# TensorE takes the instructions of one stage in traced order: attention, mLSTM and the first output projection of a two-layer hybrid backbone

## The chip, the core and the metric

The kernel runs on one core of one Trainium2 chip. The metric is device time in microseconds (us), here the median of three runs. The engines are TensorE (PE; its weight loads are shown apart as PEld), VectorE (DVE), ScalarE (ACT), GpSimd (POOL), and SyncE (SP), which issues most DMAs. All of them run at once, each through its own queue, and they wait for one another by semaphores.

## What is computed

Two layers of a hybrid backbone run over 256 context tokens and 1024 latent tokens of width 1024. Cut to what matters here, one layer is:

```python
hl = rms_norm(x_lat, norm1_g) * (1.0 + sc1) + sh1
zl = split_cols(hl @ w_in)
s5 = s5_mixer(...)
ml = mlstm_mixer(...)            # chunks of 128 tokens, both directions, 4 heads
da = diff_attention_mixer(...)   # w = softmax(s1) - lam * softmax(s2); o = w @ v
gl = gla_mixer(...)
x_lat = x_lat + g1 * (concatenate([s5, ml, da, gl]) @ w_out)
x_lat = x_lat + g2 * sq_relu_mlp(rms_norm(x_lat, norm2_g) * (1.0 + sc2) + sh2)
```

Context tokens go through the same layer, but not through the outputs of the last one.

## The kernel before, in words

The kernel is one long unrolled program, written in generators that are traced in turn. A traced instruction goes to the queue of its engine, and the scheduler of the programming layer then sets the order within each queue. It models the run, and whenever an engine comes free in its model it takes, of the instructions whose inputs are ready there, the one that was traced first. So a queue may leave the traced order wherever the model found the next traced instruction not ready. What comes out is a fixed order: on the chip each engine takes its queue from the front.

A layer has these stages: input projections, beside S5 and gated linear attention (GLA); then attention, mLSTM and the first half of the output projection, which is the stage of the change; then the second half of the output projection and the MLP.

In the stage of the change three generators are traced side by side (lines 1485 to 1499):

- `da_mix` (line 442), differential attention. For each head and each tile of 128 queries, `scores` multiplies queries by keys into PSUM (`daps`, L486), once for each of two maps and in up to three pieces of up to 512 keys. DVE takes each piece out with a running minimum (`das`, L487), ACT takes the exponential (L498), and DVE combines the two maps (L506). `values` then transposes the weights (`dapt`, L527), ACT copies them out (`dawT`, L528), and `dapo` (L518) multiplies them by the values. Score pieces go to three PSUM banks: two are called "a", the third piece has "x".
- `ml_mix` (line 690), the mLSTM. Transposes of the keys (`mlpt`, L756), state products (`mlpu`, L788), scores (`mlst`, L804), values (`mlpn`, L821 and L826), and, for each pair of chunks, `finish` (line 837): POOL and ACT and DVE normalise a tile `mlhs`, and two transposes (`mlpt`, L853) turn it. `mlhs` has one buffer.
- `p_out` (line 1465), the output projection of the S5 and GLA halves. For each 256 columns (a chunk of columns) `mix_parts` (line 1437) loads four pieces `mr` through two buffers (L1443), and ACT and DVE split each into a high part `mh` (L1444) and a low part `ml` (L1445), which have one buffer each; then eight output tiles follow, each of twelve matmuls `wop` (L1124 to L1126) whose weights `whl` are loaded and split, and each is taken out by ACT (`pg`, L1480). There are five such chunks in the first layer and four in the second.

The traced order around the change comes from two helpers. `both(da, 1, ml, 0.25)` (line 1218) traces one step of mLSTM to four steps of attention. `beside(..., po, 0.12)` (line 1135) traces one output tile, twelve `wop`, to about every eight steps of attention, and the first of them after the very first score matmul, since the credit is then already above zero. `dapt`, `wop` and the small attention products share the two PSUM banks "b".

Of the kernel before, what the change touches and what calls it, by code (L numbers as in the profile page):

```python
# [1091 lines left out]
ENG = dict(P=mybir.EngineType.PE, V=mybir.EngineType.DVE, A=mybir.EngineType.Activation, G=mybir.EngineType.Pool, S=mybir.EngineType.SP)  # L1092
# [42 lines left out]
def beside(main, filler, rate, guard=contextlib.nullcontext):  # L1135

    credit = 0.0
    for c in main:
        credit += rate * c
        if credit > 0:  # L1140
            with guard():
                while credit > 0:
                    credit -= next(filler, 1e9)
# [69 lines left out]
def both(a, na, b, nb):  # L1213

    ca = cb = 0.0
    for x in a:
        yield x
        ca += 1
        while cb / nb < ca / na:
            next(b, None)  # L1220
            cb += 1
# [44 lines left out]
def tile_hybrid_backbone(ctx: ExitStack, tc: tile.TileContext, io, out):  # L1266
# [49 lines left out]
    def pool(nm, side=None):  # L1316
        p = tc.tile_pool(name=nm, bufs=1, side=side, reuse_waits="tile") if side else tc.tile_pool(name=nm, bufs=1, reuse_waits="tile")
        return p, p.__enter__()

    def shut(p):  # L1320
        p.__exit__(None, None, None)
# [42 lines left out]
    for l in range(L):  # L1364
# [8 lines left out]
        if l == 0:  # L1373

            npc, P = pool("nx0", "right")
# [28 lines left out]
        def put(i):  # L1404
            def cb(m, t, c0):
                (nc.sync, nc.scalar, nc.sync, nc.sync)[i].dma_start(mix_d[i, m, :, c0:c0 + t.shape[1]], t)
            return cb
# [3 lines left out]
        if l == 0:  # L1411
            ready(("dak1",))
            spc, P = pool("s5p0")
# [52 lines left out]
        def p_out(P):  # L1466

            w = 256
            for b in blocks:
                t0, t1 = BLK[b]  # L1470
                for c in range(t0, t1, w):
                    n = min(w, t1 - c)
                    g1 = mod(l, 2, b == 0)
                    parts = mix_parts(P, c, n, 0, w)
                    for m in range(8):
                        x = P.tile([128, w], F32, tag="xo", name="xo", bufs=2)
                        nc.sync.dma_start(x[:, :n], x_d[:, m, c:c + n])
                        p = out_proj(m, n, 0, parts, c == BLK[blocks[0]][0])
                        pg = P.tile([128, w], F32, tag="pg", name="pg", bufs=1)
                        nc.scalar.mul(pg[:, :n], p, g1[:, m:m + 1])  # L1480
                        nc.gpsimd.tensor_tensor(x[:, :n], x[:, :n], pg[:, :n], op=ALU.add)
                        nc.sync.dma_start(xn_d[:, m, c:c + n], x[:, :n])
                        yield n / 256
# [5 lines left out]
        poc, P = pool(f"po{l}")  # L1489
        po = p_out(P)  # L1490
        da = da_mix(env, l, st, zd["dav"], io["da_lam"][l], 0.8 - 0.6 * math.exp(-0.3 * l), io["da_ng"][l], env.bones, put_da, need)
        mgc, MG = pool(f"mlg{l}", "right")
        mgates = ml_gates(env, l, MG, zd["gates"], io["ml_gb"][l], io["amask"], io["hsel"])
        ml = ml_mix(env, l, mgates, lambda i: zd[("mlq0", "mlq1", "mlk0", "mlk1")[i]], zd["mlv"], zd["mlo"], io["ml_cw"][l], io["ml_cb"][l],
                    io["ml_ng"][l], io["cmask"], put(1), need)
        beside((1 for _ in both(da, 1, ml, 0.25)), po, 0.12)
        list(ml)
        shut(mgc)
        list(po)
        env.banks.update(BANKS)  # L1500
        shut(ps2c)
        ps2c = banks(f"ps2{l}")
# [13 lines left out]
        woc, P = pool(f"wo{l}", "right")  # L1516
# [20 lines left out]
        hdc, P = pool(f"hid{l}", "right")  # L1537
# [76 lines left out]
    fnc, P = pool("fin")  # L1614
# [98 lines left out]
```

## Time and profile before

| | us |
|---|---|
| median of three runs (lowest, highest) | 3724.48 (3724.34, 3726.04) |
| the profiled execution, own time | 3719.97 |
| its span, first to last instruction | 3718.2 |
| busy: PE matmul, PE weight load | 3435.5, 2725.4 |
| busy: DVE, ACT, POOL | 2228.8, 1309.4, 450.7 |

The durations below come from the one profiled execution. Matmuls are pipelined and their ends are modelled, so a busy PE is not PE at its peak. The stage of the change runs from about 640 to 1013 us in the first layer and from about 2582 to 2915 us in the second. In rows of the timeline, "[0.80 <-DVE mlhs L849]" says that the engine stood idle for 0.80 us and what ended that.

### The profile page before, as it was taken

Reading aid. Unit: us, or ns where it says so; the run is one execution under the profiler, and the core shown is the slowest. Engines: PE = TensorE matmul, PEld = TensorE weight load, DVE = VectorE, ACT = ScalarE, POOL = GpSimd, SP = SyncE. Lnnn points to the kernel's source line nnn. Section 1 sums busy time; section 2 is a strip of 40 time slices with the busy share of each in tenths; the row PEclk is TensorE's granted clock in tenths of the full one; section 3 lists DMA queues with packets and bytes.
Section 4 is the critical chain, followed back from the end, with each engine's and each line's share of the span. In section 5 each row is a group of like instructions: output and inputs, shape, how many; then the busy total and the mean of one; then the engine's idle time right before and its main releaser. Section 6 shows DMA issues by size and latency. Waiting matters only on the chain. (4 is left out here: it accounts for less than half of the span.)

```text
span 3718.2 us, 53487 instructions
## 1 busy us (share of the span) xinstructions
PE 3435.5 (92%) x20338; PEld 2725.4 (73%) x20338; DVE 2228.8 (60%) x5455; ACT 1309.4 (35%) x2457; POOL 450.7 (12%) x520
## 2 busy tenths in 40 slices
PE   6989998798889999999999798988889899999998
PEld 3867767576658888888888476867677578888885
DVE  9654685877659855455544637486788543333334
ACT  4223434766542121212121522435676431222222
POOL 2121221222100000000000123120222000000000
PEclk8979999898899999999999998999889899999999
DMA  5665324655461221222111265314653611111112
GB/s 216 230 205 154 129 77 133 214 183 166 141 208 57 90 82 69 81 74 86 61 39 42 102 201 161 120 57 143 213 167 104 205 46 51 46 51 46 52 47 78
DMA packets 233959, 430.23 MB, mean 116 GB/s; under 512 B 47415, under 2 KB 135911, under 8 KB 233447
## 3 DMA queue, kind: packets, MB, share of 16 engines
q1 hardware_dynamic: 192806, 381.03, 31.2%
q10 hardware_dynamic: 35520, 30.52, 2.6%
q0 software_dynamic: 5376, 15.28, 1.2%
q8 instruction: 160, 2.62, 0.3%
q14 instruction: 97, 0.79, 0.1%
HBM read 316.88 MB, written 109.86 MB: 115 GB/s over the span
## 5 line engine op out<-in xcount | busy, mean ns | idle before, releaser
L1562 DVE SCALAR_TENSOR_TENSOR X<-m2p,mods,X 128x256 f32<-128x256 f32 (+1 forms) x512 | 345.7, 683 | 345.1 <-PE m2p L1126 344.6
L1115 ACT CAST whi<-raw 128x1024 fp32r<-128x1024 f32 x182 | 191.1, 1050 | 919.8 <-PE m2p L1125 638.0
L1124 PE MATMUL m2p<-hidhi,whi 128*128 128x512 f32 (+1 forms) x1280 | 473.8, 372 | 3.5 <-DVE X L1562 2.8
L1124 PE MATMUL m1p<-h2hi,whi 128*128 128x512 f32 (+1 forms) x1280 | 474.3, 371 | 0.2 <-ACT h2hi L1209 0.2
L1125 PE MATMUL m1p<-h2lo,whi 128*128 128x512 f32 (+1 forms) x1280 | 473.6, 370 | 0.0
L1125 PE MATMUL m2p<-hidlo,whi 128*128 128x512 f32 (+1 forms) x1280 | 473.1, 370 | 0.0
L1126 PE MATMUL m2p<-hidhi,wlo 128*128 128x512 f32 (+1 forms) x1280 | 472.2, 370 | 0.8 <-DVE wlo L1116 0.8
L1126 PE MATMUL m1p<-h2hi,wlo 128*128 128x512 f32 (+1 forms) x1280 | 472.6, 370 | 0.0
L1116 DVE TENSOR_TENSOR wlo<-raw,whi 128x1024 fp32r<-128x1024 f32 x182 | 224.7, 1235 | 313.2 <-ACT whi L1115 301.2
L1124 PEld LDWEIGHTS m2p<-hidhi,whi 128*128 128x128 f32 x1280 | 241.6, 189 | 59.6 <-issue 8.6
L1124 PEld LDWEIGHTS m1p<-h2hi,whi 128*128 128x128 f32 x1280 | 243.1, 190 | 46.2 <-ACT whi L1115 4.2
L1126 PEld LDWEIGHTS m2p<-hidhi,wlo 128*128 128x128 f32 x1280 | 241.2, 188 | 46.4 <-issue 3.4
L1125 PEld LDWEIGHTS m1p<-h2lo,whi 128*128 128x128 f32 x1280 | 243.4, 190 | 40.8 <-DVE h2lo L1210 0.8
L1126 PEld LDWEIGHTS m1p<-h2hi,wlo 128*128 128x128 f32 x1280 | 243.2, 190 | 40.3 <-issue 0.4
L1125 PEld LDWEIGHTS m2p<-hidlo,whi 128*128 128x128 f32 x1280 | 241.6, 189 | 42.0 <-issue 2.2
L1124 PE MATMUL zp<-hhi,whi 128*128 128x512 f32 (+1 forms) x664 | 254.2, 383 | 11.6 <-ACT zst L1237 9.6
L487 DVE TENSOR_SCALAR_CACHE_REDUCE das<-daps 128x512 f32<-128x512 f32 (+1 forms) x400 | 226.0, 589 | 58.4 <-PE daps L486 55.0
L1125 PE MATMUL zp<-hlo,whi 128*128 128x512 f32 (+1 forms) x664 | 251.2, 378 | 5.6 <-DVE hlo L1205 5.2
L1126 PE MATMUL zp<-hhi,wlo 128*128 128x512 f32 (+1 forms) x664 | 249.5, 376 | 0.0
L1576 DVE TENSOR_TENSOR rl<-rl,m1p 128x256 f32<-128x256 f32 (+1 forms) x160 | 100.8, 631 | 177.1 <-ACT rl L1575 177.1
L498 ACT ACTIVATE das<-das,danm 128x1280 f32<-128x1280 f32 x128 | 174.3, 1362 | 42.7 <-DVE danm L496 42.3
L486 PE MATMUL daps<-daqk,daqk 128*128 128x512 f32 (+1 forms) x400 | 153.3, 447 | 38.0 <-DVE das L487 36.6
(460 smaller groups left out, 6671.3 us busy)
## 6 DMA issues: line engine op xcount, KB each, us to landing
raw<-w SPq DMA_DIRECT2D x136, 512.0 KB
adaw<-ada_w SPq DMA_DIRECT2D x96, 512.0 KB
whl<-wsp SPq DMA_DIRECT2D x80, 512.0 KB
wsp<-whl SPq DMA_DIRECT2D x32, 512.0 KB
raw<-wz SPq DMA_DIRECT2D x30, 512.0 KB
daqk<-da_st SPq DMA_DIRECT2D x24, 640.0 KB
mlE<-ml_rows SPq DMA_DIRECT2D x16, 640.0 KB
xn<-xo SPq DMA_DIRECT2D x72, 128.0 KB
```

The source lines that it names most:

```text
L486: pe.matmul(p[:, 0:b - a], Q[m][:, 128 * qt:128 * qt + 128], K[m][:, a:b], start=True, stop=True)
L487: v.tensor_scalar(s[:, a:b], p[:, 0:b - a], -1.0, None, op0=ALU.mult, op1=ALU.min, accum_out=pm[:, i:i + 1])
L498: act.activation(s[:, :k1], s[:, :k1], AF.Exp, bias=nm[:, 0:1], scale=-1.0, accum_out=sm[m])
L1115: nc.scalar.copy(hi, raw)
L1116: nc.vector.tensor_tensor(lo, raw, hi.bitcast(F32), op=ALU.subtract)
L1124: pe.matmul(out, ah, bh, start=i == 0, stop=False)
L1125: pe.matmul(out, ah, bl, start=False, stop=False)
L1126: pe.matmul(out, al, bh, start=False, stop=i == n - 1)
L1562: nc.vector.scalar_tensor_tensor(X[b][:, m], p[:, :n], mod(l, 5, s)[:, m:m + 1], X[b][:, m], op0=ALU.mult, op1=ALU.add)
L1576: nc.vector.tensor_tensor(rl[:, :n], rl[:, :n], p[:, :n], op=ALU.mult)
```

## The change

The tracing of the three generators is put into a context that fixes one queue: within it, TensorE's instructions keep the order in which they are traced. Nothing is computed otherwise, and the queues of the other engines are still ordered by the scheduler.

```diff
@@ -1493,10 +1493,11 @@
-        beside((1 for _ in both(da, 1, ml, 0.25)), po, 0.12)
-        list(ml)
-        shut(mgc)
-        list(po)
+        with tc.manual_schedule(engines={ENG["P"]}):
+            beside((1 for _ in both(da, 1, ml, 0.25)), po, 0.12)
+            list(ml)
+            shut(mgc)
+            list(po)
```

`ENG["P"]` (line 1092) is TensorE. The transposes of `ml_gates` are traced ahead of the context and are outside it.

## Rows read from the trace of the kernel before

**Rows 1.** Windows view, the two stages: stretch, length, then busy us (instructions) of each engine.
```profile
640.00:1013.00 373.00, 311.50 (x2376) 244.31 (x2376) 289.47 (x949) 243.73 (x543) 81.09 (x78) 0.89 0.55 179
2582.00:2915.00 333.00, 289.08 (x2121) 225.00 (x2120) 261.50 (x826) 219.15 (x457) 75.46 (x64) 0.87 0.53 173
```
**Rows 2.** Waits of DVE, first layer's stage, then second's: us in total, times, longest.
```profile
DVE das L487 <- PE daps L486: 32.4, 37, 2.8
...
DVE das L487 <- PE daps L486: 22.6, 25, 2.8
```
**Rows 3.** Waits of PE, first layer's stage (two rows), then second's.
```profile
PE daps L486 <- DVE das L487: 23.5, 18, 6.4
PE mlpu L788 <- issue: 11.0, 1, 11.0
...
PE daps L486 <- DVE das L487: 13.2, 14, 7.6
```
**Rows 4.** Timeline of PE at both starts: start, us, instruction, [idle before].
```profile
657.02 1.01 PE L486 MATMUL daps<-daqk,daqk 128*128 128x256 f32 x3
...
668.08 0.41 PE L1124 MATMUL wop<-mh,whl 128*128 128x256 f32 x1
...
2592.31 1.42 PE L486 MATMUL daps<-daqk,daqk 128*128 128x512 f32 x3
...
2602.63 0.41 PE L1124 MATMUL wop<-mh,whl 128*128 128x256 f32 x1
...
2607.37 0.58 PE L1125 MATMUL wop<-ml,whl 128*128 128x256 f32 x1 [0.86 <-DVE ml L1445]
```
**Rows 5.** Timeline of SP at the second layer's start: the issue of the pieces `mr`.
```profile
2591.17 1.15 SPq L1443 DMA_DIRECT2D mr<-mix  x2
...
2600.93 0.80 SPq L1443 DMA_DIRECT2D mr<-mix  x2
```
**Rows 6.** Windows view, starts: all engines (PE, PEld, DVE, ACT, POOL, PEclk); L487 alone; L506 alone.
```profile
2592.00:2607.40 15.40, 12.32 (x32) 7.77 (x32) 15.40 (x63) 11.90 (x28) 1.42 (x2) 0.50 0.94 308
...
657.00:668.00 11.00, 2.39 (x10) 0.50 0.43 150
2592.00:2607.40 15.40, 7.19 (x24) 0.50 0.94 308
...
657.00:668.00 11.00, 3.35 (x2) 0.50 0.43 150
```
**Rows 7.** Timeline of PE, first and last `wop` of two groups: a chunk's first, and its second.
```profile
720.30 0.39 PE L1124 MATMUL wop<-mh,whl 128*128 128x256 f32 x1
...
728.63 0.28 PE L1126 MATMUL wop<-mh,whl 128*128 128x256 f32 x1
...
729.29 0.39 PE L1124 MATMUL wop<-mh,whl 128*128 128x256 f32 x1
...
730.69 0.28 PE L1126 MATMUL wop<-mh,whl 128*128 128x256 f32 x1
```
**Rows 8.** Lines view of the whole run: combining on DVE, `dawT` on ACT.
```profile
L506 DVE SCALAR_TENSOR_TENSOR das<-das,dars 128x1280 f32<-128x1280 f32 (+1 forms) x72 | 111.5, 1549 | 0.5
...
L528 ACT COPY dawT<-dapt 128x512 f32<-128x512 f32 (+1 forms) x200 | 97.8, 505 | 65.6 <-PE dapt L527 65.1
```
**Rows 9.** Timeline of PE, the ends of both stages.
```profile
993.27 0.36 PE L486 MATMUL daps<-daqk,daqk 128*128 128x256 f32 x1
...
995.43 0.44 PE L853 MATMUL mlpt<-ident,mlhs 128*128 128x128 f32 x2 [0.80 <-DVE mlhs L849]
...
1003.04 0.44 PE L853 MATMUL mlpt<-ident,mlhs 128*128 128x128 f32 x2
...
2894.11 0.36 PE L486 MATMUL daps<-daqk,daqk 128*128 128x256 f32 x1
...
2898.29 0.44 PE L853 MATMUL mlpt<-ident,mlhs 128*128 128x128 f32 x2
```
**Rows 10.** Timeline of POOL, end of the first stage.
```profile
995.95 0.72 POOL L841 TENSOR_TENSOR mlhs<-mltmp 128x256 f32<-128x256 f32 x1 [5.04 <-PE mlpt L853]
```

## The prediction
> **What bounds the kernel now.** I read the page first, then the windows of the two stages that the change touches, then the waits of DVE and PE in them, and last the timelines of both starts and both ends. The two stages last 373 and 333 us, 706 of 3718.2, and only they can move. The reader is to see there that no engine is full [rows 1]: DVE is busy for 78% in both (289.47 of 373.00, 261.50 of 333.00), PE for 84 and 87% by its matmuls and 65 and 68% by its weight loads, ACT for 59 and 66%. So the stage is held by hand-overs. The waits name the largest one from both sides. DVE waits 32.4 and 22.6 us for a score piece from PE [rows 2], and PE waits 23.5 and 13.2 us for DVE to free a score bank [rows 3]. The two work through three banks: whatever keeps PE from its next `daps` longer than DVE has stored work costs time.
>
> **What the change does, step by step.** It adds and removes no instruction and no DMA. It fixes the order of one queue, so its price is what PE then waits for at the head of its queue, and who starves behind it. Before, an instruction that was not ready in the scheduler's model was passed over; now PE stands at it. I look for places where the traced next instruction is late for a reason that PE can't shorten.
>
> *Start of the stage.* By the code, the traced order is one `daps`, then the first twelve `wop`, then eight `daps`. Before, the scheduler put the scores first: from 657.02 us up to the first `wop` at 668.08, and from 2592.31 up to 2602.63 [rows 4]; DVE took out five pieces in the first of these stretches and twelve by 2607.4 (L487 counts 10 and 24, two instructions to a piece [rows 6]). That `wop` group can't come early. Four pieces `mr` pass through two buffers, so the second pair is issued only after the first is split, at 2600.93 after 2591.17 [rows 5], and the group still waited for a low part at 2607.37 [rows 4]. With the change PE issues one `daps` and stands there until about 668 and 2607. DVE loses what it did meanwhile: 2.39 us of L487 and 3.35 of L506 in the first layer, 7.19 of L487 [rows 6] and one combine of 1.55 [rows 8] in the second, together 14.5 us. In the second start DVE was busy for 15.40 of 15.40 us [rows 6], so nothing else of DVE's stands ready to fill all of it. Bounds: 0 if mLSTM preparation fills it, 14.5 if nothing does. DVE has some idle time later to make part good, so I take two thirds: **+10 us**. The granted clock is 0.50 there [rows 6] in any case.
>
> *First tile of each later chunk.* The parts `mh` and `ml` have one buffer, so the first group of a chunk has to wait for the last group of the one before, for loads and for splits. The first such group took from 720.30 to 728.63, with other work issued between its matmuls, the next, whole, from 729.29 to 730.69 [rows 7]: 8.3 us against 1.4. There are four such groups in the first layer and three in the second. With the change nothing is issued in between, so PE stands for up to 6.9 us. DVE has cover: up to three pieces in the banks, 3 x 0.61 us with their overlap (from 7.19 us over twelve pieces [rows 6]: 0.60), and one combine of 1.55 [rows 8], 3.4 us in all. Bounds: 0 (the eight steps of attention traced between two groups give the chain time to finish), and 7 x (6.9 - 3.4) = 24.5. I take **+10 us**, a little under the middle, because part of the 8.3 us was PE and ACT being busy with the work in between.
>
> *End of the stage.* The last two `finish` steps are traced next to each other, four attention steps apart, ahead of the last scores. Before, the last score piece went at 993.27 and the two pairs of transposes later, at 995.43 and 1003.04; the second layer shows the same, 2894.11 ahead of 2898.29 [rows 9]. The second pair can't follow the first quickly: `mlhs` has one buffer, and the POOL addition that fills it again waited for the first transposes and started at 995.95 [rows 10], so 7.6 us lie between the pairs [rows 9]. In traced order, last scores are queued behind both. The four steps of attention between them cost PE 1 to 2 us, so it stands for about 6, and behind the last scores hang exponential, combine, transposes and the end of the stage, with nothing left to fill. That is **+6 us** a layer, **+12**. Bounds: 0 if the mLSTM chain comes early enough, 2 x 10 if the first pair is also waited for.
>
> *Everything between.* Transposes, `wop` and small products share two banks that ACT empties, 200 copies of 0.505 us [rows 8]. Before, a late copy was bridged by other instructions. Upper bound: half of the copies, one per pair of banks, uncovered, 100 x 0.505 = 50 us. Lower bound: PE's waits at instructions placed too early go, 23.5 + 11.0 + 13.2 = 48 us [rows 3]. DVE at 78% [rows 1] lets neither be had in full, and the traced order gives DVE its six pieces together, which is neither better nor worse for it: 0.
>
> The sum is 10 + 10 + 12 = +32 us on the profiled execution's own 3719.97 us. The median of the runs lies 4.5 us above that execution, 3724.48, so I forecast 3756.
>
> Weighed against a page: the weight loads leave PE idle for 35 and 32% of the stages [rows 1], 129 and 108 us. The Trainium skill, in "Trainium Kernel Development and Optimization", Performance Expectations, says that matmul busy time is a bad measure and weight-load busy share a good one; the trace agrees in that the two differ here. By that alone PE has room to swallow 32 us of standing, and the sum would be 0. The room is spread between hand-overs, which is why I give that case the smaller chance.
>
> **The rivals.** *Absorbed.* PE's standing falls into time in which DVE works off stored pieces, and what is late at the start is made good by DVE's idle 22%. For it: the idle shares [rows 1]. Against it: DVE was full at the second start [rows 6], and the ends have nothing behind them [rows 9]. Time: 3724.5. The same time comes out if the order hardly changes, which is possible, since the scheduler also ranks by traced order; against that speak the scores ahead of the first `wop` and the split group [rows 4, 7].
>
> *Faster.* The scheduler's model misjudged readiness: PE stood 11.0 us at one `mlpu` that it had been given too early, and up to 6.4 us at a `daps` [rows 3], with earlier traced work behind it. In traced order this work comes first. If half of the 48 us goes and the three terms above come to nothing, the time is 3724.5 - 24 = 3700. It decides at the point where the traced next instruction is ready more often than the model's pick, and DVE's wait for `daps` falls below its 55 us [rows 2].
>
> *Much slower.* The bank copies are not covered, +50 on top: 3806.
>
> **How the numbers follow.** The forecast with its three terms has a chance of 0.5, much slower 0.1, absorbed or unchanged 0.14, faster 0.26. Two runs of this kernel can be told apart from about 0.2%, 7.4 us. So faster 0.26, same 0.14, slower 0.60. The range reaches from 3708, where about half of the faster case is left out, up to 3806, the three terms with the uncovered copies.
>
> **What would show it.** Right: in the profile after, the first `wop` follows the first `daps`, with PE idle for some 10 us ahead of it in both layers; waits of `wop` L1124 to L1126 for `mh`, `ml` or `whl` reach several us at chunk starts; `mlpt` L853 stands ahead of the last `daps` with a wait of some 6 us; DVE's wait for `daps` rises above 55 us; both stages are longer, by 16 us each or so, and the rest of the run is as long as before. Wrong: PE's waits for `das` and `mlpu` gone and DVE's wait for `daps` lower; or the first `wop` ready soon after the first `daps`, because SP then issues `mr` earlier.

## The result, and the profile after

The changed kernel takes 3863.0 us (median of 4 runs, 3857.79 to 3866.17), the kernel before 3724.4 us beside it (4 runs, 3714.79 to 3726.04). The ratio is 1.0376, with a 95% interval from 1.0354 to 1.0398: 140 us slower, where 32 were forecast and the range ended at 3806. In all that follows, a loss in us is (ratio - 1) x 3724, with the interval worked out in the same way; here it is 132 to 148. The expectations below reckon with differences of medians and so differ from the tables by a few us.

The profiled execution took 3865.28 us, its span is 3863.5. First the windows view of the two stages. The stretches run from the first to the last take-out of a score piece by DVE (L487), so that they cover the same work in both kernels: 208 pieces in the first layer, 192 in the second. Columns: stretch, length, then busy us (instructions) of PE, PEld, DVE, ACT and POOL, granted clock, DMA share, GB/s. The kernel before:

```profile
657.60:994.10 336.50, 297.86 (x2285) 234.53 (x2284) 270.06 (x912) 217.64 (x491) 78.22 (x76) 0.92 0.53 170
2593.10:2897.10 304.00, 273.57 (x2019) 213.88 (x2018) 246.73 (x795) 199.50 (x420) 72.91 (x62) 0.88 0.54 174
```

and the changed kernel, same view:

```profile
659.80:1077.00 417.20, 312.19 (x2270) 249.37 (x2271) 286.41 (x925) 227.08 (x507) 81.20 (x77) 0.83 0.45 144
2674.20:3043.50 369.30, 268.71 (x2013) 214.72 (x2015) 256.13 (x800) 201.45 (x421) 68.65 (x63) 0.84 0.45 145
```

The stretches are longer by 80.7 and 65.3 us, together 146.0; the spans differ by 145.3. So the whole loss lies between the first score and the last. The busy time of PE rises by only 9 us (571.4 to 580.9), its idle time from 69.1 to 205.6 and DVE's from 123.7 to 244.0. The engines do nearly the same work and wait for one another. DVE's busy time is 26 us longer (516.8 to 542.5) on 18 more instructions, which wasn't followed up. The granted clock, here the mean of a stretch, falls from 0.92 and 0.88 to 0.83 and 0.84.

Next, DVE's waits in the changed kernel, first the stage of layer 0, then that of layer 1 (us in total, times, longest); the first row of each answers to [rows 2]:

```profile
DVE das L487 <- PE daps L486: 55.6, 42, 4.7
DVE dars L505 <- ACT das L498: 25.1, 27, 3.3
...
DVE das L487 <- PE daps L486: 47.1, 35, 4.7
DVE dars L505 <- ACT das L498: 26.6, 22, 2.3
```

The wait for a score piece rose from 55.0 us to 102.7. The second row of each was small in the kernel before:

```profile
DVE dars L505 <- ACT das L498: 3.0, 6, 1.2
...
DVE dars L505 <- ACT das L498: 6.5, 8, 1.5
```

DVE now stands 51.7 us at the combine of two maps, for ACT's exponential. That wait is not in my prediction at all. The exponential comes late mainly because its scores do: it needs the minimum that DVE makes of a map's pieces (`danm`, L496), and ACT's own wait for that doubled from 42.3 us to 85.0. From the end of the minimum to the start of its exponential no more time passes than before, 0.54 us in the mean against 0.77. ACT's wait in both layers of the kernel before, then in both of the changed kernel:

```profile
ACT das L498 <- DVE danm L496: 19.4, 13, 7.3
...
ACT das L498 <- DVE danm L496: 22.9, 18, 6.5
```

```profile
ACT das L498 <- DVE danm L496: 42.5, 19, 5.1
...
ACT das L498 <- DVE danm L496: 42.5, 22, 6.4
```

PE's waits in the changed kernel, same columns, with layer 0 first; the `daps` rows answer to [rows 3]:

```profile
PE dapt L527 <- ACT dawT L528: 13.8, 15, 2.2
...
PE dams L552 <- ACT dasq L550: 12.1, 7, 2.4
PE wop L1124 <- ACT mh L1444: 11.6, 8, 3.1
PE daps L486 <- DVE das L487: 10.3, 24, 1.3
PE dapo L518 <- ACT dawT L528: 10.1, 9, 3.3
...
PE dapt L527 <- ACT pg L1480: 6.1, 7, 2.6
...
PE daps L486 <- DVE das L487: 18.1, 26, 3.0
...
PE mlpt L853 <- DVE mlhs L849: 11.2, 3, 5.2
PE dapt L527 <- ACT dawT L528: 10.5, 10, 3.6
...
PE dams L552 <- ACT dasq L550: 7.5, 3, 3.0
...
PE dapt L527 <- ACT pg L1480: 5.6, 5, 4.1
...
PE dapo L518 <- ACT dawT L528: 3.2, 5, 1.0
```

The waits that the old order had are smaller, as the "faster" rival said: `daps` for `das` went from 36.7 to 28.4 us, and the 11.0 us at an `mlpu` are gone. In their place stand many small ones, none of the rows shown here over 5.2 us (two longer ones stand at the starts of the stages and are shown further below: 11.8 us for the first operands `daqk`, ahead of the first score, and 8.2 us at the first `wop` of layer 1). A transpose or a product waits for a copy of ACT, `dams` for its square, `mlpt` for mLSTM's rows. The two rows of `dapt` and the one of `dapo` sum to 49.3 us; before, the same three were 9.0:

```profile
PE dapt L527 <- ACT pg L1480: 3.8, 3, 2.6
...
PE dapo L518 <- ACT dawT L528: 1.3, 4, 0.6
...
PE dapt L527 <- ACT dawT L528: 0.7, 2, 0.4
...
PE dapt L527 <- ACT dawT L528: 1.3, 4, 0.4
PE dapo L518 <- ACT dawT L528: 1.3, 3, 0.7
...
PE dapt L527 <- ACT pg L1480: 0.6, 2, 0.3
```

How such a place looks is read from PE's timeline of the changed kernel in layer 0 (some rows are left out, among them those of L1125 and L1126, the other two thirds of each `wop` triple):

```profile
809.79 0.39 PE L486 MATMUL daps<-daqk,daqk 128*128 128x256 f32 x1 [1.28 <-DVE das L487]
...
812.21 0.43 PE L518 MATMUL dapo<-dawT,davt 128*64 128x128 f32 x2 [0.58 <-ACT dawT L528]
813.83 0.66 PE L518 MATMUL dapo<-dawT,davt 128*64 128x128 f32 x6 [1.18 <-ACT dawT L528]
...
818.28 0.58 PE L1124 MATMUL wop<-mh,whl 128*128 128x256 f32 x1 [1.05 <-ACT mh L1444]
819.33 1.27 PE L486 MATMUL daps<-daqk,daqk 128*128 128x512 f32 x3
```

Between two score bursts PE stands three times for something that ACT makes, 2.8 us in all, and the `wop` in the same gap opens a chunk, whose `mh` is late. 9.5 us pass from one `daps` to the next. DVE and ACT in the same stretch:

```profile
813.55 0.27 DVE L505 TENSOR_SCALAR dars<-dars,nlam,dark 128x1 f32<-128x1 f32 x1 [1.45 <-ACT das L498]
...
820.00 0.69 DVE L487 TENSOR_SCALAR_CACHE_REDUCE das<-daps 128x512 f32<-128x512 f32 x1 [1.31 <-PE daps L486]
```

```profile
817.82 0.40 ACT L1444 CAST mh<-mr 128x256 fp32r<-128x256 f32 x1 [2.03 <-DMA mr<-mix]
```

DVE waits for ACT's exponential, ACT for the load of a piece `mr`, PE for ACT's copies and its high part `mh`, and DVE at last for PE's scores. All three score banks were empty from 811.4 us on; the next scores only had their place in the queue against them.

The loss isn't made at a few places. This table counts score pieces from the first of the stage, which is number 0 and stands at time 0 in both kernels, and gives how many us later than in the kernel before the n-th is taken out:

```
layer 0, n      16    32    48    64    80    96   112   128   160   207
changed        8.0  12.2  21.5  34.4  42.1  38.5  48.6  61.2  78.6  80.7
layer 1, n      16    32    48    64    80    96   112   128   160   191
changed        1.1  19.0  18.3  31.5  39.5  42.6  58.4  55.1  59.6  65.4
```

### The profile page after: what moved, and what is told of

Same layout as the page of the kernel before. It is cut to its first block, busy times and chain, and to the rows that moved or that the text cites. A ratio compares the mean times of both kernels' runs of the same rounds, so it can differ in the third digit from the quotient of the medians.

```text
span 3863.5 us, 53452 instructions
## 1 busy us (share of the span) xinstructions
PE 3449.0 (89%) x20338; PEld 2744.0 (71%) x20338; DVE 2251.2 (58%) x5455; ACT 1316.3 (34%) x2457; POOL 446.9 (12%) x520
## 5 line engine op out<-in xcount | busy, mean ns | idle before, releaser
L1124 PE MATMUL m2p<-hidhi,whi 128*128 128x512 f32 (+1 forms) x1280 | 473.7, 372 | 4.1 <-DVE X L1563 3.4
L1124 PE MATMUL m1p<-h2hi,whi 128*128 128x512 f32 (+1 forms) x1280 | 475.7, 372 | 0.2 <-ACT h2hi L1209 0.2
L1125 PE MATMUL m1p<-h2lo,whi 128*128 128x512 f32 (+1 forms) x1280 | 474.8, 371 | 0.0
L1126 PE MATMUL m1p<-h2hi,wlo 128*128 128x512 f32 (+1 forms) x1280 | 473.8, 370 | 0.0
L1125 PE MATMUL m2p<-hidlo,whi 128*128 128x512 f32 (+1 forms) x1280 | 473.2, 370 | 0.0
L1126 PE MATMUL m2p<-hidhi,wlo 128*128 128x512 f32 (+1 forms) x1280 | 472.4, 370 | 0.8 <-DVE wlo L1116 0.8
L1124 PEld LDWEIGHTS m2p<-hidhi,whi 128*128 128x128 f32 x1280 | 241.8, 189 | 60.2 <-issue 8.6
L487 DVE TENSOR_SCALAR_CACHE_REDUCE das<-daps 128x512 f32<-128x512 f32 (+1 forms) x400 | 222.0, 590 | 103.5 <-PE daps L486 102.6
L1124 PEld LDWEIGHTS m1p<-h2hi,whi 128*128 128x128 f32 x1280 | 244.2, 191 | 46.3 <-ACT whi L1115 4.2
L1126 PEld LDWEIGHTS m2p<-hidhi,wlo 128*128 128x128 f32 x1280 | 241.3, 189 | 46.4 <-issue 3.4
L1125 PEld LDWEIGHTS m1p<-h2lo,whi 128*128 128x128 f32 x1280 | 244.4, 191 | 40.9 <-DVE h2lo L1210 0.6
L1126 PEld LDWEIGHTS m1p<-h2hi,wlo 128*128 128x128 f32 x1280 | 244.3, 191 | 40.4 <-issue 0.4
L1125 PEld LDWEIGHTS m2p<-hidlo,whi 128*128 128x128 f32 x1280 | 241.6, 189 | 42.0 <-issue 2.2
L1124 PE MATMUL zp<-hhi,whi 128*128 128x512 f32 (+1 forms) x664 | 255.7, 385 | 11.1 <-ACT zst L1237 9.6
L1125 PE MATMUL zp<-hlo,whi 128*128 128x512 f32 (+1 forms) x664 | 252.4, 380 | 5.6 <-DVE hlo L1205 5.2
L1126 PE MATMUL zp<-hhi,wlo 128*128 128x512 f32 (+1 forms) x664 | 251.0, 378 | 0.0
L1124 PE MATMUL wop<-mh,whl 128*128 128x256 f32 (+1 forms) x448 | 164.3, 367 | 70.2 <-ACT mh L1444 34.6
```

The lines of the kernel that those rows point to most:

```text
L487: v.tensor_scalar(s[:, a:b], p[:, 0:b - a], -1.0, None, op0=ALU.mult, op1=ALU.min, accum_out=pm[:, i:i + 1])
L1124: pe.matmul(out, ah, bh, start=i == 0, stop=False)
L1125: pe.matmul(out, ah, bl, start=False, stop=False)
L1126: pe.matmul(out, al, bh, start=False, stop=i == n - 1)
```

## The experiments

**Which sequence's order costs.** In place of the one region, the instructions of a chosen sequence (attention, mLSTM, projection) are tied together in the order in which they are traced; sequences that aren't tied stay the scheduler's. By the code, one chain over all three would be the changed kernel's order; that wasn't run. Of the lines with a run's label each run has its own; NO_SYNC stands for a dependency that orders and waits for nothing.

```diff
-        with tc.manual_schedule(engines={ENG["P"]}):
-            beside((1 for _ in both(da, 1, ml, 0.25)), po, 0.12)
+        def chain(gen, tail):
...
+                for i in bb[k:]:
+                    if i.engine == ENG["P"]:
+                        if tail:
+                            tc.add_manual_dep(i, tail[0].name, NO_SYNC, reason="chain")
+                        tail[:] = [i]
...
+        da, ml, po = chain(da, []), chain(ml, []), chain(po, [])    # a1
+        t = []; da, ml = chain(da, t), chain(ml, t)                 # a2
+        t = []; da, po = chain(da, t), chain(po, t)                 # a3
+        da = chain(da, [])                                          # b1
+        po = chain(po, [])                                          # b2
+        ml = chain(ml, [])                                          # b3
+        beside((1 for _ in both(da, 1, ml, 0.25)), po, 0.12)
```

Run a4 keeps the region, but only around `list(ml)`, `shut(mgc)` and `list(po)`.

Own order of each (a1):

> TensorE's instructions of attention, of mLSTM and of the projection each keep their traced order, but the three sequences are free against one another (three chains in place of one). Theory 1 (the loss comes from the fixed mixture: PE stands at the head of its queue for a late operand of one sequence while another sequence is ready): nearly all of the 139 us goes, 3725 to 3745 us, and PE's idle time in the two stages falls from 234 us back to about 110. Theory 2 (the order inside one sequence costs: transposes that stand behind late copies, dams behind its square, head changes that wait for daqk, the two finish steps): most of the loss stays, 3830 us or more.

Projection free (a2):

> Attention and mLSTM in one traced order, the projection (wop) free against them. In the changed kernel PE's idle time ahead of wop L1124 to L1126 rose from 0.4 to 28.5 us in layer 0 and from 9 to about 26 in layer 1. Theory 1a (the fixed place of the wop groups, which wait for parts and weights with single buffers, makes most of the loss): 3760 us or less. Theory 1b (the loss is spread over all hand-overs and wop's share is what its own waits show, 45 us): 3810 to 3825. Theory 2: 3840 or more.

mLSTM free (a3):

> Attention and the projection in one traced order, mLSTM free against them. PE's waits at mlpt, mlpu, mlst and mlpn in the changed kernel sum to about 20 to 30 us over both layers, the last two finish steps among them with 5.5 us in layer 0. Theory 1a: 3840 us or more. Theory 1b: 3830 to 3845. Theory 3 (mLSTM's chain is what makes PE stand; its copies queue behind the others on ACT): 3780 or less.

Only what is traced behind the interleaved part (a4):

> The fixed order covers only what is traced after the interleaved part (the rest of mLSTM and of the projection); attention with its neighbours is scheduled as before. Prices the end of the stages by itself. By the forecast's term for the end alone, +12 us, which lies inside the interleaved part: 3724 here, plus or minus 5. If the projection's remainder loses by its order (PE waits for whl and mh behind the stage), 3735 or more.

Attention alone (b1):

> Only attention's TensorE instructions keep their traced order; mLSTM and the projection are scheduled. With each of the three in its own order the loss was 55 us of 139. Theory P (the projection's own order makes it: its groups wait for mh and ml with one buffer, 38 us of PE's waits there): here 3720 to 3735. Theory A (attention's bursts: six scores, then transposes behind their copies): 3750 or more.

Projection alone (b2):

> Only wop keeps its traced order. Theory P: 3755 or more. Theory A: 3735 or less. My term for the first tile of each later chunk (+10, bounds 0 to 24.5) and the part of the start that wop makes by itself would both show here; by them 3719 + 10 = 3729 to 3740.

mLSTM alone (b3):

> Only mLSTM's TensorE instructions keep their traced order. In the run with three own orders PE stood 38 us ahead of mlpu, 19 of it for mlkw; in the kernel before 13.5. Theory M (mLSTM's own order is part of the 55): 3735 to 3745. Theories P and A: 3719 to 3730.

Measured:

```
tied together                       time      ratio (95%)               loss, us
projection                 (b2)   3720.5   0.9996 (0.9980, 1.0011)       -1
mLSTM                      (b3)   3726.3   1.0018 (1.0005, 1.0031)        7
attention                  (b1)   3752.5   1.0085 (1.0057, 1.0112)       32
each by itself             (a1)   3773.9   1.0138 (1.0114, 1.0163)       51
attention + projection     (a3)   3800.5   1.0211 (1.0183, 1.0239)       79
attention + mLSTM          (a2)   3814.9   1.0261 (1.0229, 1.0292)       97
all three, as changed             3863.0   1.0376 (1.0354, 1.0398)      140
behind the interleaved part (a4)  3715.2   0.9992 (0.9975, 1.0008)       -3
```

A good third of the loss, 51 us, is there when every sequence only keeps its own order, and 32 of it is attention's. Theory P fell: the projection's own order is free. a1 came out between its two theories, a2 where theory 1b put it, a3 better than 1b and worse than theory 3. b2 missed the 3729 to 3740 us that my terms for the first groups put there: the projection's fixed order costs nothing as long as the other two may fill its gaps. Fixing mLSTM's place against attention adds 46 us (97 - 51), fixing the projection's adds 28 (79 - 51), both to within some 15; mLSTM has no order at all in a3, and its own is worth 7 (b3), so the 28 is rather too low. 51 + 46 + 28 = 125, and what joining all three adds beyond the two joints, 15 us, isn't clear of noise. Neither theory 1 nor theory 2 held alone; the two share the loss. Nothing is lost behind the interleaved part (a4 is at 0 within its interval, and 4 us below its range). Line view of PE's idle time in a1, over both stages and some work around them (count, busy and mean | idle before and its releasers), shows most of the mixture's waits gone and some of attention's own left:

```profile
L527 PE MATMUL dapt<-ident,das 128*128 128x128 f32 x656 | 111.6, 301 | 38.6 <-DVE das L506 16.6 <-ACT dawT L528 12.8 <-DVE dark L541 2.8
...
L518 PE MATMUL dapo<-dawT,davt 128*64 128x128 f32 x1312 | 112.1, 301 | 3.1 <-ACT dawT L528 2.9
...
L853 PE MATMUL mlpt<-ident,mlhs 128*128 128x128 f32 x36 | 8.0, 303 | 4.6 <-DVE mltmp L835 3.5 <-DVE mlhs L849 0.8 <-DVE dars L504 0.3
```

**Whether the traced order can be mended.** These keep the region of the changed kernel, with all of TensorE in traced order, and change the order in which the program traces. First, spread scores:

```diff
-                        yield from scores(Qs, Ks, pr[z], k1, rs[...])
-                        yield from drain(5 + z)
+                        for j, x in enumerate(scores(Qs, Ks, pr[z], k1, rs[...])):
+                            yield x
+                            if j + 6 * z > 2:
+                                yield from drain(1)
+                    yield from drain(2)
```

b4:

> All in traced order as in the changed kernel, but the program traces attention differently: from the fourth score piece of a pair of tiles on, each daps is followed by one step of the values (transposes or products) of the pair before, in place of six daps and then five or six steps. Theory A (the burst order makes PE stand at late copies and DVE starve between bursts): PE's waits at dapt and dapo for dawT (24 and 13 us in the changed kernel) and DVE's for daps (103 us) fall by half, 3800 us or less. Theory B (what costs is the mixture with the two other sequences): 3845 to 3865. If each daps then waits for DVE with the transposes queued behind it: above 3870.

A later first group, for my term at the start (c1):

```diff
-            beside((1 for _ in both(da, 1, ml, 0.25)), po, 0.12)
+            beside((k > 9 for k, _ in enumerate(both(da, 1, ml, 0.25))), po, 0.12)
```

c1:

> The changed kernel, except that the first ten steps of the main sequence earn no credit for the projection, so its first twelve wop are traced behind the first eight scores. My term for the start was +10 us (bounds 0 to 14.5); the changed kernel's trace shows PE standing 7.1 us at these wop in layer 0 and 8.2 in layer 1 right behind the first daps. If the term holds, 3853 us (3849 to 3858); if DVE makes it good later, 3863.

The projection only behind the third score piece of a tile: the steps of attention earn credit for it there and nowhere else (c2).

```diff
                     late_at -= 1
-                    yield 1
+                    yield 11.5 * npc / 3 if m == 1 and i == npc - 1 else 0
...
-                    yield 1
+                    yield 0
...
-            beside((1 for _ in both(da, 1, ml, 0.25)), po, 0.12)
+            beside(both(da, 1, ml, 0.25), po, 0.12)
```

c2:

> The changed kernel, except that a projection group is traced only behind the third score piece of a tile, in the middle of its six daps, and no longer among the transposes. Theory S (the two banks that dapt and wop share make the cost of mixing the projection in: 27 us more with it in the joint order than with its own): waits of dapt for pg (12 us) and of wop for dawT (5 us) go, 3835 to 3850. If the place in the tile is indifferent: 3858 to 3868.

Both finish steps cut in two (c3): a step ends behind attention's square and behind mLSTM's last product, and `drain` returns at the first of these.

```diff
             act.activation(sq, o, AF.Square)
+            yield 2
             pms = env.bank("dat", "dams")
...
-                    if not n:
+                    if not n or x == 2:
                         return
...
+                yield 1
                 mo = env.wp.tile([128, 512], F32, tag="zst", name="mlmo", bufs=2)
```

c3:

> The changed kernel, except that both finish steps are cut in two: attention's between dapr and dams with six scores traced in between, mLSTM's between the additions and the transposes mlpt with four attention steps in between. In the changed kernel PE waits 19.6 us ahead of dams and some 29 us ahead of mlpt L853. Theory H (PE standing at the head of its queue behind a chain through ACT, POOL and DVE is the loss, and it adds up): 3815 to 3835. If such a wait falls into time that is lost anyway: 3850 or more. My term for the end of the stage (+12) is part of it.

Four loads of a chunk at once, for my term at the chunk starts (e1). TensorE's order is the changed kernel's, row for row.

```diff
-                mr = env.wp.tile([128, 512], F32, tag="zst", name="mr", bufs=2)
+                mr = env.wp.tile([128, w], F32, tag="zst", name="mr", bufs=1024 // w)
...
-                mo = env.wp.tile([128, 512], F32, tag="zst", name="mlmo", bufs=2)
+                mo = env.wp.tile([128, 256], F32, tag="zst", name="mlmo", bufs=4)
```

e1:

> The changed kernel with four buffers of 256 columns for the pieces mr (and mlmo) in the same memory as the two of 512, so all four loads of a chunk are issued at once; TensorE's order is the same. The chunk starts show some 19 us of PE's waits in the changed kernel over both layers, my term was +10. If the pieces' two buffers make it: 3845 to 3856. If it is the single buffer of mh and ml, or the wait costs nothing: 3858 to 3868.

c2 and c3 together, with the operands of the map that is scored first also loaded first (c4):

```diff
-            for hm in (2 * h, 2 * h + 1):
+            for hm in (2 * h + 1, 2 * h):
...
-                    L_.append(tl)
+                    L_.insert(0, tl)
```

c4:

> The changed kernel with the projection behind the scores, both finish steps cut in two, and the score operands of the map that is used first loaded first. Theory H: the parts add up, 3785 to 3815. If the loss is not in named places: 3840 or more.

b4, c1 and c3 together, with four empty steps ahead of `dams` and `drain(3)` at the end of a pair (d2):

d2:

> The changed kernel (all of TensorE in traced order) with every mend of the traced order: value steps spread among the scores, both finish steps cut, the first wop ten steps later. Theory H (named places that add up): 3863 less 32, 22 and 35 = 3774. Theory M (the mends take the same loss from different sides): 3800 to 3830. If the fixed order as such costs nothing: 3730 or less.

And mLSTM traced faster, `both(da, 1, ml, 0.4)` (d4):

d4:

> The changed kernel with mLSTM traced at 0.4 steps to a step of attention in place of 0.25. Theory E (joining mLSTM costs because it stands too late in the traced order, and PE and DVE lack its work early on): 3845 or less, with the stage's score progress closer to that of before. Theory N (its place is indifferent): 3855 to 3870. If its late operands then hold attention up more often: above 3875.

Measured, with the gain against the changed kernel's 140 us:

```
all in traced order, and            time     ratio (95%)             loss   gain
scores spread              (b4)   3830.8   1.0292 (1.0265, 1.0320)    109     31
first wop ten steps later  (c1)   3827.8   1.0284 (1.0262, 1.0306)    106     34
projection behind scores   (c2)   3839.9   1.0315 (1.0291, 1.0339)    117     23
finish steps cut           (c3)   3840.5   1.0318 (1.0285, 1.0350)    118     22
four mr                    (e1)   3841.3   1.0322 (1.0297, 1.0346)    120     20
c2 + c3 + loads turned     (c4)   3812.0   1.0235 (1.0213, 1.0257)     88     52
b4 + c1 + c3               (d2)   3796.5   1.0207 (1.0180, 1.0234)     77     63
mLSTM traced earlier       (d4)   3902.1   1.0486 (1.0457, 1.0515)    181    -41
```

Five different mends give 20 to 34 us each, to within some 12 to 15, and each takes away a hand-over at which PE stood. Others grow in its place. In b4 PE's waits of `dapt` and `dapo` for `dawT` fell from 37.6 to 2.5 us, as theory A had it, but those at `dams` rose from 19.6 to 52.6, and DVE's for `daps` stayed at 103.7. In c3 the waits at `dams` fell to 5.6, and `dapt` for `dawT` rose from 24.3 to 46.8. In c2 the named waits fell (`dapt` for `pg` from 11.7 to 4.3), and `wop` for `whl` rose from 17.4 to 40.3. c2 and c4 came out where they were expected with theories S and H; b4, c3 and d2 lie between their theories, and e1 and c1 came out below their ranges, on the good side. So theory H is right that these waits are on the path. Theory M, that the mends overlap, is likely for b4, c1 and c3, which sum to 87 and together give 63, though these 24 us are about the noise of such a sum; c2 and c3 sum to 45, and together, with the loads turned as well, they give 52. The count of score pieces of c1 tells where: by piece 16 it is 4.2 and 4.0 us ahead of the changed kernel (3.8 and -2.9 against 8.0 and 1.1), which is the start, and by the last one 25 and 8 us. So three quarters of its gain came later in the stage, where the groups now stand elsewhere in every tile; which hand-overs gave it wasn't followed up. d4 goes against theory E and came out as its third case: with mLSTM earlier PE waits more often for its operands (`mlpu` for `mlkw` 9 times and 30.0 us, 3 times and 6.2 in the changed kernel), and the loss grows to 181.

What d2 still loses, 77 us, shows as PE standing, as this windows view of d2 shows; stretches and columns as above:

```profile
655.00:1048.80 393.80, 301.51 (x2284) 242.89 (x2284) 280.95 (x912) 227.86 (x503) 81.89 (x75) 0.83 0.45 145
2648.50:2977.30 328.80, 259.78 (x2015) 209.30 (x2015) 246.47 (x789) 202.26 (x418) 69.02 (x61) 0.84 0.48 152
```

PE is idle for 161.3 us in 722.6, against 205.6 in 786.5 (changed) and 69.1 in 640.5 (before).

One rival is left untested. With PE's order fixed, the scheduler also orders the queues of DVE and ACT anew: in the traces the take-outs and copies follow one another differently from the first rows of the stage on. No run fixes those orders, so how much of the 140 us is theirs is open.

**Whether any fixed order of attention costs.** d1 ties attention alone, as b1 does, with the spread order and four scores ahead of `dams`; d3 takes that tracing without any tie.

d1:

> Only attention in its own traced order (as in b1, which lost 34 us), but traced with the value steps spread among the scores and with four score pieces between dapr and dams. Theory A1 (the bursts and the finish step are what costs in attention's own order): 3719 to 3732. Theory A2 (any fixed order of attention costs, because the scheduler's order follows the readiness of transposes and copies, which shifts from tile to tile): 3745 or more.

d3:

> The kernel before, all order left to the scheduler, with the program tracing attention spread and its finish cut. If the traced order only steers ties for the scheduler: 3715 to 3730. If the order of scores in six suits DVE better: 3735 or more. If alternating serves DVE better also here: 3705 or less.

d1 takes 3748.3 us, ratio 1.0081 (1.0051, 1.0111), 30 us: about b1's 32, and in the range of theory A2. But d3 takes 3740.6, 1.0057 (1.0035, 1.0079): 21 us slower than before, with no tie at all. The traced order also matters where the scheduler is free, and spread scores are worse there. So most of d1's loss is the spread tracing itself, and tying attention adds only 9 us to it, with an uncertainty of some 14, where it adds 32 to the tracing in bursts (b1). Neither theory is settled by this: theory A1's time fell, but the tie may well cost less with spread scores, and A2's reason wasn't tested. Once all of TensorE is in traced order, spreading the scores gains 31 us (b4).

**A mend for the kernel before.** e2 is the kernel before with the loads turned round, as in c4.

e2:

> The kernel before with the score operands of the second map of a head loaded first, since its scores are traced first. If attention's first scores come earlier by the 14 us of PE's wait that this took away in the changed kernel and DVE, which is full at the start, gains from it: 3705 to 3716. If something else has PE and DVE busy until then: 3719 to 3728.

It takes 3733.6 us, 1.0030 (1.0010, 1.0049): 11 us slower, outside both expectations. PE waits 25 us for `daqk` in the changed kernel, most of it ahead of the first scores, but no such wait shows in the kernel before, so there was none to take away; why turning the loads round costs anything wasn't followed up. No version here beats the kernel before by more than the noise.

## Why the prediction was wrong

The sign was right and the size four times too small. By its steps:

**Start of the stage, +10: right in place, and in size only over both layers.** Timeline of PE in the changed kernel, the first scores and the first `wop` of both layers (most `wop` rows left out):

```profile
656.46 0.55 PE L486 MATMUL daps<-daqk,daqk 128*128 128x256 f32 x1 [11.85 <-DMA daqk<-da_st]
662.95 0.58 PE L1124 MATMUL wop<-mh,whl 128*128 128x256 f32 x1 [5.94 <-ACT whl L1456]
...
668.22 0.63 PE L486 MATMUL daps<-daqk,daqk 128*128 128x256 f32 x2
...
2670.91 0.77 PE L486 MATMUL daps<-daqk,daqk 128*128 128x512 f32 x1 [7.69 <-DMA daqk<-da_st]
2679.92 0.58 PE L1124 MATMUL wop<-mh,whl 128*128 128x256 f32 x1 [8.24 <-ACT whl L1456]
...
2683.32 1.27 PE L486 MATMUL daps<-daqk,daqk 128*128 128x512 f32 x3
```

One `daps`, then 11.8 and 12.4 us until the next, as the step said. Take-out 16 is 8.0 and 1.1 us late, 9.1 together, and c1 gave 8.2 of it back. That the sum is met is in part luck: by layers the step allowed for at most 5.7 and 8.7 us, so layer 0 lost more than its bound, and layer 1 made nearly all of it good, although DVE had looked full there.

**First tile of each later chunk, +10: right in place, too small.** PE stands at the seven such groups for 0.6 to 7.6 us, 19 us in all, as in the example at 818.28. e1 gave 20 us back (by its interval, 11 to 29 against 140), inside the bounds of 0 to 24.5; it also gave `mlmo` more buffers, so the 20 may not be `mr`'s alone. The term needs the other sequences tied too: with only the projection in its own order (b2) nothing is lost.

**End of the stage, +12: right in place and wait, somewhat too large.** The ends of the changed kernel on PE's timeline:

```profile
1070.44 0.41 PE L853 MATMUL mlpt<-ident,mlhs 128*128 128x128 f32 x2 [1.72 <-DVE mlhs L849]
...
1076.12 0.66 PE L853 MATMUL mlpt<-ident,mlhs 128*128 128x128 f32 x2 [3.75 <-DVE mlhs L849]
1076.43 0.56 PE L486 MATMUL daps<-daqk,daqk 128*128 128x256 f32 x1
...
3027.90 0.66 PE L853 MATMUL mlpt<-ident,mlhs 128*128 128x128 f32 x2 [2.85 <-DVE dars L504]
...
3036.12 0.66 PE L853 MATMUL mlpt<-ident,mlhs 128*128 128x128 f32 x2 [5.21 <-DVE mlhs L849]
...
3040.11 0.85 PE L486 MATMUL daps<-daqk,daqk 128*128 128x512 f32 x3
```

Both pairs of transposes stand ahead of the last scores, where before they came behind [rows 9], and PE waits 5.5 and 8.1 us at them, for the 6 that the step took. How much of it reaches the end is bounded by the table of score pieces: from piece 160 to the last the delay grows by 2.1 us in layer 0 (78.6 to 80.7) and by 5.8 in layer 1 (59.6 to 65.4), 8 us with everything else that happens there. c3, with 22 us for all finish steps, doesn't part the last ones from the rest.

**Everything between, 0: this step failed.** As far as they can be measured, the three terms are 9, 20 and 8 us, 37; about 100 of the 140 lie in what I took as nothing. Two faults stand in it. Its upper bound counted only the bank copies, 50 us. The waits of `dapt` and `dapo` for ACT rose by 40.3 us (9.0 to 49.3), close to that, but by luck: they are 51 waits of 0.97 us in the mean, not 100 of 0.505. Beyond them, `dams` behind its own square (4.2 to 19.6 us), mLSTM's transposes all along the stage (`mlpt` L853: 2.0 to 29.0, of which 13.5 are the end) and `wop` behind parts and weights belong to it too, and outside the three places none of these has a term. The same "instruction at the head of the queue" that I priced at three named places stands at every tile. And its value was taken from a symmetry that isn't there. I set the gains at PE's old waits (48 us) against these losses and took 0, because DVE at 78% would let neither be had in full. In fact 19.3 us of the old waits went, and PE's idle time still rose by 136.5. DVE's idle time nearly doubled, and it now also stands at the combine (51.7 us, 9.5 before), since late scores make late exponentials.

One row is misread without an effect on the sum: ACT is busy for 65% of the first stage (243.73 of 373.00 [rows 1]), not 59.

**The rivals.** Absorbed and faster fell. The "faster" mechanism is there, at its point (`mlpu`, `daps` for `das`), and is smaller than what comes in its place. Much slower was the right direction, with one of the right causes, and ended at 3806. The absorbed case leaned on the Trainium skill, "Trainium Kernel Development and Optimization", Performance Expectations, which calls the weight-load busy share a good measure of how close a kernel is to the roofline, the best time the chip allows. That idle weight loads are room for standing was the prediction's own step from it. The trace disagrees with that step, with weight loads busy for 70% of both stretches before (234.53 of 336.5, 213.88 of 304.0), for 60 and 58% now, and 140 us lost.

What stays open is why a fixed order of attention alone costs 32 us (b1), and why d2, with the starts, the finish steps and the bursts mended, still loses 77. That the scheduler's placement differs from tile to tile, because mLSTM and the projection fall differently beside each, fits, and isn't shown.

## What to carry to other kernels

When a queue that three sequences share is put into a fixed order, price every hand-over at which the queue can stand, tile by tile, and not only the ends: here the three named places hold some 37 us, about what was forecast, and the rest about 100. A way to do this, not tried here, is to count, in the trace of before, all instructions that were issued between a producer's late result and its consumer; that filler is what the fixed order takes away. And tie the sequences one by one and then in pairs: the losses (32, then 51, then 46 and 28 more) tell which freedom pays; the waits by themselves don't, since one that is taken away comes back in part at another place (b4, c2, c3).

## What was not expected of the hardware

With more idle time of PE the granted clock was lower: 0.92 and 0.88 over the two stretches before, 0.83 and 0.84 after, at almost the same count of instructions. In layer 0 the `wop` of L1124 took 325 ns in the mean before and 355 after:

```profile
L1124 PE MATMUL wop<-mh,whl 128*128 128x256 f32 x160 | 51.5, 325 | 0.4 <-ACT pg L1480 0.3
```

```profile
L1124 PE MATMUL wop<-mh,whl 128*128 128x256 f32 (+1 forms) x163 | 57.8, 355 | 23.7 <-ACT mh L1444 11.6 <-ACT whl L1456 5.9 <-DMA whl<-wsp 3.8
```

The (+1 forms) are three rows with 512 columns behind the stage, too few to make the difference. So standing may cost a little twice, but this isn't shown: in layer 1 the same matmuls took 334 ns in the mean before and 331 after, in spite of the lower clock, and PE's busy time rose by 14 us in layer 0's stretch and fell by 5 in layer 1's.
